# Fourteen Strassen groups instead of ten in each feed-forward part, and half of the ordinary low halves summed by DMAs

## The chip, the cores and the metric

The kernel runs on one core of a Trainium2 chip. It is written in Python against the engines: PE (TensorE) multiplies, PEld loads its stationary operand, DVE (VectorE) and ACT (ScalarE) do elementwise work, POOL (GpSimd) does a little of it and can begin DMAs, SP (SyncE) begins all other DMAs. Engines run their own instruction lists in order and wait for each other through semaphores. The metric is the device time of one execution in microseconds (us), lower is better.

## The reference

The reference is a two-layer block on 256 tokens of 2048 features in float32. Each layer has a mixer (the first a convolution and pooling mixer, the second a short-convolution mixer) and a feed-forward part:

```python
def swiglu(h, w_gate, w_up, w_down):
    return (jax.nn.silu(h @ w_gate) * (h @ w_up)) @ w_down

def reference(...):
    h = x
    for i in range(DEPTH):                       # DEPTH = 2
        ...                                      # mixer i
        h = h + swiglu(rms_norm(h, ffn_norm[i]), w_gate[i], w_up[i], w_down[i])
    return rms_norm(h, final_norm)
```

`w_gate` and `w_up` are 2048 x 5632, `w_down` is 5632 x 2048. The two feed-forward parts hold most of the arithmetic, and the change touches only them.

## The kernel before

**Three matmuls for one.** Weights are float32. PE multiplies a reduced format (`float32r`), so each operand is cut in two: a high half (the value rounded to that format) and a low half (the value less its high half). A product is three matmuls of 256 columns: high by high, high by the low of the other, low by high. ACT writes a weight's high half (`nc.scalar.copy`, line 200), and the low half is a subtraction (line 201), done by DVE, or by POOL for some pieces of the first mixer. The activations' halves are made once, in `split`.

**Units, pieces, tokens.** All weights lie in one array in the order in which they are used. A weight block is 128 x 128. SP loads units of 16 blocks, 1 MB, into four staging buffers `w` (pool `wst`, `fetch`, line 189). A unit of the ordinary kind ("P") is cut into pieces of 8 blocks, and `prepare` makes the two halves of a piece into the pool `whl`, which has five buffers named `hi` and five named `lo`. `advance` is called once for each token (one block's product, or one Strassen step): it prepares the pieces of the next three tokens that begin a piece (`LOOK`), and fetches one unit beyond.

**Strassen groups.** The 44 chunks (128 columns each) of gate and up are computed in two ways. An ordinary chunk takes 16 blocks of gate and 16 of up, three matmuls a block. A group takes two chunks, both of gate and up, by a seven-product scheme over 2 x 2 quarters: four units of weights, 14 steps each, three matmuls a step (lines 742 to 744, into the banks `s0` to `s3`). Of such a unit ("S") four parts are prepared (512, then three times 1024 columns), and DVE also makes three combinations of the quarters in place (lines 225 to 227). At the end of a product `combine` adds up the banks on DVE, and at the end of a group `turned` turns the result back with four transposes on PE (line 697) and writes it to `y`. The combinations of the activations are made at the start of a part by `s_forms`, from `h` through a tile `form` into `sf`.

**Sections and windows.** The 44 chunks are done in six sections, `SECTIONS`: pairs of (groups, ordinary chunks). In window w, section w of gate and up is computed, and the down projection of section w - 1 runs beside it; `merged` lays the steps of a window among its ordinary blocks in runs of 14. A seventh window holds the last section's down projection alone. With ten groups a part has 1472 ordinary blocks and 560 steps.

**What sets the order.** The program is written token by token, and a list scheduler then orders each engine's instructions; so an engine's order differs from the program's. A buffer of a pool is free when its last reader is done, and whoever fills it next waits for that: ACT waits for PE before it writes a `hi`, SP waits for DVE before it loads a `w`.

## Time and profile before

| | |
|---|---|
| median of 3 runs | 2032.01 us (2030.86 to 2033.54) |
| the profiled execution | 2031.89 us, its span 2030.0 us |
| PE, DVE, ACT, POOL busy | 98%, 82%, 56%, 10% of the span |
| mean granted clock of PE | 0.995 |
| bytes read from HBM | 391.39 MB, 194 GB/s over the span |
| feed-forward parts | about 250 to 941 us and 1306 to 1998 us |

In the rows of the trace, a line such as `L201 DVE ... x768 | 936.3, 1235 | 219.5 <-ACT hi L200` gives the line of the kernel, the engine, the operation, what is written from what, how many times, then the busy us and the mean ns of one, then the idle us of the engine just before them and who ended most of it. The rows of a stage give for each engine its busy us and the number of its instructions, then the granted clock, the mean busy share of the 16 DMA engines, and GB/s. Rows of DMA issues give the size of one and the median time from issue to landing. In the order of an engine's instructions a row has the line, the operation, what is written from what with buffer numbers, the size, and in brackets the semaphores it waits for (PE_49 is PE's, DMAHW those of DMAs begun by SP, DMASW those of DMAs begun by POOL).

### The profile page before, as it was taken

The page shows a single profiled execution, that of the slowest core. Times are in us where ns is not written, and L with a number is a line of the kernel's source. Part 1 is how long each engine was busy: PE and PEld are TensorE (multiplying, and loading weights), DVE is VectorE, ACT ScalarE, POOL GpSimd, SP SyncE. Part 2 cuts the span into 40 slices and gives each one's busy share as a digit, 9 for nine tenths or more (in the row PEclk, how much of TensorE's full clock was granted, in tenths as well). Part 3 has the DMA queues.
Part 4 walks back from the last instruction along what each step waited for, and adds up shares of the span by engine and source line. Part 5 has one row for each costly group of instructions (what it writes and reads, how often), then busy time and mean ns, then how long its engine had stood idle before and what let it go on. Part 6 is the DMA issues. An engine that isn't in the chain of part 4 may idle for free.

```text
span 2030.0 us, 41535 instructions
## 1 busy us (share of the span) xinstructions
PE 1996.3 (98%) x17410; PEld 1989.2 (98%) x17410; DVE 1664.1 (82%) x2326; ACT 1129.0 (56%) x1476; POOL 194.5 (10%) x180
## 2 busy tenths in 40 slices
PE   8999999999999999999999999999999999999997
PEld 8999899999999999999999999999999999999997
DVE  6998787888888888888766666788888888889875
ACT  7786675555555555556444445565555555555545
POOL 2996200000000000002000001100000000000002
PEclk9999999999999999999999999999999999999999
DMA  8555445454555545555555555545455454555552
GB/s 332 188 185 192 149 176 198 175 220 187 208 208 183 212 185 210 208 197 186 200 187 196 200 188 195 200 166 209 186 204 213 183 213 186 204 191 198 216 188 83
DMA packets 56922, 396.15 MB, mean 195 GB/s; under 512 B 6432, under 2 KB 7200, under 8 KB 9760
## 3 DMA queue, kind: packets, MB, share of 16 engines
q1 hardware_dynamic: 56736, 393.52, 52.5%
q8 instruction: 136, 2.23, 0.4%
q14 instruction: 50, 0.41, 0.1%
HBM read 391.39 MB, written 2.10 MB: 194 GB/s over the span
## 4 chain that ended last, share of the span: by engine, by line
PE 90%; DVE 7%; ACT 1%; DMA 1%; issue 1%; SPq 0%; POOL 0%; DVEq 0%; ACTq 0%; POOLq 0%
PE acc L289 24%; PE acc L290 23%; PE acc L291 23%; PE s L744 6%; PE s L742 6%; PE s L743 6%; DVE lo L201 2%; DVE side L513 1%; DVE side L515 1%; PE acc L697 0%; DMA rows<-in_xtok 0%; DMA h<-in_xT 0%; DVE h L782 0%; DVE xs L316 0%; ACT hi L200 0%
## 5 line engine op out<-in xcount | busy, mean ns | idle before, releaser
L200 ACT CAST hi<-w 128x1024 fp32r<-128x1024 f32 (+2 forms) x900 | 897.2, 1012 | 746.3 <-PE acc L290 431.9
L201 DVE TENSOR_TENSOR lo<-w,hi 128x1024 fp32r<-128x1024 f32 (+2 forms) x851 | 989.5, 1181 | 237.4 <-ACT hi L200 222.3
L289 PE MATMUL acc<-xs,hi 128*128 128x256 f32 x2816 | 777.2, 277 | 5.3 <-ACT hi L200 4.2
L290 PE MATMUL acc<-xs,hi 128*128 128x256 f32 x2816 | 775.7, 276 | 0.0
L291 PE MATMUL acc<-xs,lo 128*128 128x256 f32 x2816 | 772.7, 276 | 0.1
L289 PEld LDWEIGHTS acc<-xs,hi 128*128 128x128 f32 x2816 | 529.6, 188 | 6.2 <-ACT hi L200 4.8
L290 PEld LDWEIGHTS acc<-xs,hi 128*128 128x128 f32 x2816 | 529.8, 188 | 0.1
L291 PEld LDWEIGHTS acc<-xs,lo 128*128 128x128 f32 x2816 | 527.6, 188 | 0.6 <-DVE lo L201 0.5
L289 PE MATMUL acc<-y,hi 128*128 128x256 f32 x1408 | 389.0, 277 | 1.7 <-ACT y L699 1.3
L290 PE MATMUL acc<-y,hi 128*128 128x256 f32 x1408 | 388.2, 276 | 0.4 <-DVE y L700 0.4
L291 PE MATMUL acc<-y,lo 128*128 128x256 f32 x1408 | 386.7, 275 | 0.0
L289 PEld LDWEIGHTS acc<-y,hi 128*128 128x128 f32 x1408 | 264.2, 188 | 2.9 <-ACT y L699 1.8
L290 PEld LDWEIGHTS acc<-y,hi 128*128 128x128 f32 x1408 | 264.4, 188 | 0.9 <-DVE y L700 0.9
L291 PEld LDWEIGHTS acc<-y,lo 128*128 128x128 f32 x1408 | 263.9, 188 | 0.0
L422 POOL TENSOR_TENSOR sumsq<-sumsq,sq 128x256 f32<-128x256 f32 x56 | 52.6, 939 | 1553.1 <-ACT sq L420 1552.6
L743 PE MATMUL s<-hi,sf 128*128 128x256 f32 x640 | 175.7, 275 | 0.0
L742 PE MATMUL s<-hi,sf 128*128 128x256 f32 x640 | 175.7, 275 | 0.0
L744 PE MATMUL s<-lo,sf 128*128 128x256 f32 x640 | 171.8, 276 | 0.0
L744 PE MATMUL s<-lo,xs 128*128 128x256 f32 x480 | 132.5, 276 | 2.4 <-DVE lo L201 2.4
L742 PE MATMUL s<-hi,xs 128*128 128x256 f32 x480 | 132.6, 276 | 1.3 <-ACT hi L200 1.3
L743 PE MATMUL s<-hi,xs 128*128 128x256 f32 x480 | 132.2, 275 | 0.0
L201 POOL TENSOR_TENSOR lo<-w,hi 128x1024 fp32r<-128x1024 f32 x49 | 119.7, 2466 | 37.6 <-ACT hi L200 36.7
(163 smaller groups left out, 2310.4 us busy)
## 6 DMA issues: line engine op xcount, KB each, us to landing
w<-in_wall SPq DMA_DIRECT2D x365, 1024.0 KB, 4.9
w<-in_wall SPq DMA_DIRECT2D x7, 512.0 KB, 7.9
rows<-in_xtok SPq DMA_DIRECT2D x2, 1024.0 KB, 7.8
h<-in_xT SPq DMA_DIRECT2D x7, 256.0 KB, 7.2
out<-res SPq DMA_DIRECT2D x2, 512.0 KB, 2.8
out<-res SPq DMA_DIRECT2D x2, 384.0 KB, 2.7
v<-in_vec SPq DMA_DIRECT2D x1, 260.0 KB, 6.6
h<-in_xT SPq DMA_DIRECT2D x2, 128.0 KB, 2.3
```

Of the source, the lines that this page charges most:

```text
L200: nc.scalar.copy(hi, src)
L201: engine.tensor_tensor(out=lo, in0=src, in1=hi, op=ALU.subtract)
L289: nc.tensor.matmul(acc, hi, x[:, :T], start=first, stop=False)
L290: nc.tensor.matmul(acc, hi, x[:, T:], start=False, stop=False)
L291: nc.tensor.matmul(acc, lo, x[:, :T], start=False, stop=last)
L422: nc.gpsimd.tensor_tensor(out=self.sums[0], in0=self.sums[0], in1=sq, op=ALU.add)
L513: nc.vector.scalar_tensor_tensor(out=dst, in0=src, scalar=wt, in1=dst, op0=ALU.mult, op1=ALU.add)
L515: nc.vector.tensor_tensor(out=side, in0=side, in1=prods.pop((c, k)), op=ALU.add)
L742: nc.tensor.matmul(acc, xh, hi, start=first, stop=False, skip_group_check=True)
L743: nc.tensor.matmul(acc, xl, hi, start=False, stop=False, skip_group_check=True)
L744: nc.tensor.matmul(acc, xh, lo, start=False, stop=last, skip_group_check=True)
```

## The change

Four things change together, all in the feed-forward parts:

- `SECTIONS` holds 14 groups and 16 ordinary chunks in place of 10 and 24, in sections of 7, 5, 8, 8, 8 and 8 chunks. A part has 1216 ordinary blocks and 784 steps.
- Of each ordinary unit of 16 blocks that begins within a stated range of a part (`SUMMED`: from its 49th token to the end of its sixth window), the second piece gets its low half in another way. When the first piece is prepared, ACT writes minus the rounded weights into the `lo` buffer (`AF.Copy`, scale -1), and POOL begins a DMA that adds the weights to it (`accum_op=ALU.add`). The high half is cast when the piece itself is due. There are 65 such units in each part, 130 in all; the other low halves stay as they were.
- There are six `lo` buffers in place of five (also for the pieces of the first mixer that had a low buffer of their own).
- `s_forms` uses a quarter of one `w` staging buffer for each of its tiles, in place of the tile `form`.

```diff
-SECTIONS = ((1, 8), (2, 2), (2, 6), (2, 2), (2, 4), (1, 2))
+SECTIONS = ((1, 5), (2, 1), (2, 4), (3, 2), (3, 2), (3, 2))
...
+FFN_TOKENS = sum(len(w) for w in WINDOW_KINDS)
+SUMMED = sum(len(w) for w in WINDOW_KINDS[:-1])
+SUMMED = [range(at + 48, at + SUMMED) for at in (M0_BLOCKS, M0_BLOCKS + FFN_TOKENS + M1_BLOCKS)]
...
-    relief = []
+    relief, early = [], {}
...
         if spare:
-            hi, lo = (banks["spare"].tile([P, W_ROOM], F32R, name=x)[:, SPARE_AT : SPARE_AT + n] for x in ("hi", "lo"))
+            hi = banks["spare"].tile([P, W_ROOM], F32R, name="hi")[:, SPARE_AT : SPARE_AT + n]
         else:
-            hi, lo = (whl.tile([P, W_ROOM], F32R, name=x)[:, at : at + n] for x in ("hi", "lo"))
+            hi = whl.tile([P, W_ROOM], F32R, name="hi")[:, at : at + n]
+        lo = whl.tile([P, W_ROOM], F32R, name="lo", bufs=6)[:, at : at + n]
         nc.scalar.copy(hi, src)
         engine.tensor_tensor(out=lo, in0=src, in1=hi, op=ALU.subtract)
...
-            ready[key] = halves_of(w[:, o * P : (o + n) * P], 0, n * P, engine, key[1] in SPARE and i % 6 == 5)
+            src = w[:, o * P : (o + n) * P]
+            if u in early:
+                hi = whl.tile([P, W_ROOM], F32R, name="hi")[:, : n * P]
+                nc.scalar.copy(hi, src)
+                ready[key] = hi, early.pop(u)
+                return
+            if o == 0 and UNITS[u][3] == 2 * PIECE and any(UNITS[u][0] in x for x in SUMMED):
+                early[u] = lo = whl.tile([P, W_ROOM], F32R, name="lo", bufs=6)[:, : PIECE * P]
+                nc.scalar.activation(lo, w[:, PIECE * P :], AF.Copy, scale=-1.0)
+                nc.gpsimd.dma_start(lo, w[:, PIECE * P :], accum_op=ALU.add)
+            ready[key] = halves_of(src, 0, n * P, engine, key[1] in SPARE and i % 6 == 5)
             return
...
-    def s_forms(room, norm, fp, k):
-
-        f = fp.tile([P, 4, P], F32, name="form")
+    def s_forms(room, norm, scratch, k):
+
+        f = scratch[:, k % 4 * 4 * P : (k % 4 + 1) * 4 * P].rearrange("p (q t) -> p q t", q=4)
...
+            scratch = wst.tile([P, 16 * P], F32, name="w")
             for k in range(8):
-                later("wait", "form", partial(s_forms, sf, norm, fp, k))
+                later("wait", "form", partial(s_forms, sf, norm, scratch, k))
```

In the changed file the subtraction stands on line 205, the negation on 232, the DMA on 233, the three matmuls of a block on 303 to 305 and those of a Strassen step on 757 to 759.

## The prediction

> **What bounds the kernel now.** I read the head of the page first, then the chain that ended last, then the busy time by stage (the two feed-forward parts are 250 to 941 and 1306 to 1998 us, with the short-convolution mixer between them).

> ```profile
> span 2030.0 us, 41535 instructions
> PE 1996.3 (98%) x17410; PEld 1989.2 (98%) x17410; DVE 1664.1 (82%) x2326; ACT 1129.0 (56%) x1476; POOL 194.5 (10%) x180
> PE 90%; DVE 7%; ACT 1%; DMA 1%; issue 1%; SPq 0%; POOL 0%; DVEq 0%; ACTq 0%; POOLq 0%
> ```

> ```profile
> core 0: us, PE busy (x) PEld busy (x) DVE busy (x) ACT busy (x) POOL busy (x), PEclk, DMA share, GB/s
> 250.00:941.00 691.00, 687.12 (x6022) 685.27 (x6021) 591.27 (x793) 379.69 (x459) 1.99 (x2) 1.00 0.53 198
> 941.00:1306.00 365.00, 364.68 (x3206) 363.86 (x3206) 256.80 (x346) 170.17 (x213) 28.01 (x43) 1.00 0.54 191
> 1306.00:1998.00 692.00, 688.41 (x6036) 686.81 (x6036) 592.22 (x792) 378.86 (x461) 1.53 (x2) 1.00 0.53 195
> 430.00:600.00 170.00, 170.00 (x1498) 170.00 (x1497) 145.11 (x183) 92.79 (x109) 0.00 (x0) 1.00 0.54 200
> ```

> PE is the bound: 90% of the last chain, and idle for 4 us of each feed-forward part. In the undisturbed stretch of the last row a matmul takes a turn every 170/1498 = 0.1135 us. So the number of matmuls sets these parts, as long as nothing that a matmul reads comes late. DVE has about 14% to spare there (591 of 691), ACT 45%, POOL is empty, and the 16 DMA engines are half busy. The profiled execution took 2031.89 us; its span is 2030.0, and 1.9 us lie around it. It is within 0.2 us of the median of the runs, so the sum is made on 2031.9.

> **The change, part by part.**

> (1) Matmuls. A group does two chunks of gate and up in 56 steps x 3 = 168 matmuls, where the ordinary way takes 2 x 2 x 16 x 3 = 192. Four more groups in each part, eight in all, remove 8 x 24 = 192 matmuls: 192 x 0.1135 = **-21.8 us**. Each group adds four transposes, in two pairs:

> ```profile
> 622.93 0.28 PE L744 MATMUL s<-lo,sf 128*128 128x256 f32 x1
> 623.05 0.38 PE L697 MATMUL acc<-v 128*128 128x128 f32 x2
> 623.19 0.36 PE L289 MATMUL acc<-xs,hi 128*128 128x256 f32 x1
> 623.39 0.28 PE L290 MATMUL acc<-xs,hi 128*128 128x256 f32 x1
> ```

> From 623.05 to 623.39 a pair and one matmul take 0.34; less the matmul's 0.11 a pair costs 0.23. 16 pairs are **+3.7 us**. PE alone would thus gain 18.1 us.

> (2) DVE. The rows that price it (and ACT):

> ```profile
> L201 DVE TENSOR_TENSOR lo<-w,hi 128x1024 fp32r<-128x1024 f32 x768 | 936.3, 1235 | 219.5 <-ACT hi L200 205.2
> L200 ACT CAST hi<-w 128x1024 fp32r<-128x1024 f32 x817 | 846.6, 1052 | 681.2 <-PE acc L290 399.5 <-DVE w L227 190.1 <-PE s L743 64.9
> L225 DVE TENSOR_TENSOR w<-w 128x1024 f32<-128x1024 f32 x80 | 97.5, 1219 | 1.1
> L201 DVE TENSOR_TENSOR lo<-w,hi 128x512 fp32r<-128x512 f32 x81 | 55.6, 687 | 17.2 <-ACT hi L200 16.3
> L226 DVE TENSOR_TENSOR w<-w 128x512 f32<-128x512 f32 x80 | 54.8, 685 | 0.9
> L200 ACT CAST hi<-w 128x512 fp32r<-128x512 f32 x81 | 50.4, 622 | 64.4 <-PE acc L290 32.3 <-DMA w<-in_wall 21.8 <-issue 5.5
> L443 DVE TENSOR_TENSOR gate<-acc,rstd 128x256 f32<-128x256 f32 x72 | 30.3, 421 | 17.5 <-PE acc L291 17.3
> L700 DVE TENSOR_TENSOR y<-acc,y 128x512 fp32r<-128x512 f32 x20 | 13.7, 684 | 2.3 <-ACT y L699 2.3
> L724 DVE SCALAR_TENSOR_TENSOR v<-v,rtok,c 128x256 f32<-128x256 f32 x20 | 9.5, 476 | 0.0
> L708 DVE TENSOR_TENSOR c<-s,a 128x256 f32<-128x256 f32 x20 | 8.3, 417 | 0.0
> ```

> A Strassen unit costs DVE 3 x 1.235 + 0.687 + 1.219 + 2 x 0.685 = 6.98 us; 32 more units are +223. Eight more groups add seven sums of 0.42, two products of 0.48 and a 0.68 each, +36. Removed are 64 low halves of ordinary pieces that no longer exist and the 130 that DMAs now sum, 194 x 1.235 = -240, and four operations of 0.42 for each of 16 ordinary chunks, -27. The sum is -8 us: DVE is as full as before. Without the DMAs it would be 161 us fuller, of some 200 that it is idle in both parts, and in the last three sections 137 us of its rows would stand against 122.6 us of matmuls; the DMAs are the cover under which the matmuls may be dropped. With them, DVE has 122 us of rows there for the 1080 matmuls of a section; rows of DVE overlap by about 0.08, and the same sum for a middle section of before gives 110 of 114 where the stages show 86% busy, so I expect 90%. ACT gains 130 negations (as a cast, 1.05) and the units' casts, about 195 us on 1129: not a bound. Of DVE's bursts at the turn of a group I expect what is there now, under 1 us at some turns; I leave it at nothing in the sum and 4 us in the range.

> (3) The new chain: ACT negates half a unit, POOL begins a DMA, the DMA reads the half and the negation and writes the sum, PE waits. POOL's order in the change, at the start of the second part (L436 is the running sum of squares, L233 the DMA):

> ```order
> L436 TENSOR_TENSOR sumsq_15454<-sumsq_15454,sq_16363 128x256 [waits Activation_49,Pool_49]
> L233 DMA lo_16575<-w_16479 128x1024 [waits DMASW2_49,DMAHW3_49,DVE_49,Activation_49]
> L233 DMA lo_16656<-w_16582 128x1024 [waits DMASW3_49,DMAHW4_49,DVE_49,Activation_49]
> L233 DMA lo_16743<-w_16663 128x1024 [waits DMASW7_49,DMAHW5_49,DVE_49,Activation_49]
> L233 DMA lo_16906<-w_16812 128x1024 [waits DMASW4_49,DMASW0_49,DMAHW7_49,DVE_49,Activation_49]
> ```

> Where POOL stood empty there are now 65 DMAs in each part and nothing else among them, so a DMA waits on POOL for nobody; the issue also has no queue of SP to pass. What matters is how long the chain may take. ACT in the fifth section of the second part, change:

> ```order
> L204 CAST hi_21901<-w_21811 128x1024 [waits DMAHW2_49,PE_49,Activation_49]
> L227 CAST hi_21919<-w_21811 128x1024 [waits PE_49,Activation_49]
> L204 CAST hi_21933<-w_21905 128x512 [waits DMAHW3_49,PE_49]
> L232 ACTIVATE lo_21898<-w_21811 128x1024 [waits DMASW1_49]
> L783 ACTIVATE gate_21884<-gate_21884 128x256 [waits DVE_49]
> ```

> and before, at a like place (an ordinary unit's two casts between the casts of Strassen units):

> ```order
> L200 CAST hi_21258<-w_21155 128x1024 [waits DMAHW5_49,PE_49,Activation_49]
> L200 CAST hi_21276<-w_21155 128x1024 [waits DVE_49,PE_49]
> L200 CAST hi_21304<-w_21262 128x512 [waits DMAHW6_49,DVE_49,PE_49]
> L200 CAST hi_21336<-w_21262 128x1024 [waits PE_49]
> L200 CAST hi_21369<-w_21262 128x1024 [waits DVE_49,PE_49,Activation_49]
> ```

> The negation stands behind three casts, the first of which waits for a buffer. There are five buffers of high halves, and the one it gets is that of `hi_21793`. PE in the change frees it in the third row here:

> ```order
> L305 MATMUL acc_21761<-xs_75,lo_21772 128x256
> L303 MATMUL acc_21761<-xs_75,hi_21793 128x256
> L304 MATMUL acc_21761<-xs_75,hi_21793 128x256
> L305 MATMUL acc_21761<-xs_75,lo_21772 128x256
> L757 MATMUL s1_21635<-hi_21856,sf_16435 128x256 [waits Activation_49]
> ```

> and needs the sum 70 matmuls later, in the fourth row here:

> ```order
> L757 MATMUL s1_21635<-hi_21951,sf_16435 128x256
> L758 MATMUL s1_21635<-hi_21951,sf_16435 128x256
> L759 MATMUL s1_21635<-lo_21952,sf_16435 128x256
> L305 MATMUL acc_21887<-xs_75,lo_21898 128x256 [waits DMASW5_49]
> L303 MATMUL acc_21887<-xs_75,hi_21919 128x256
> ```

> PE works in order, so everything behind that row stands while it waits. That ACT is tied to freed buffers, and how soon it starts, the trace shows (the wait's total, and one instance):

> ```profile
> ACT hi L200 <- PE acc L290: 431.9, 324, 4.0
> 505.16 0.28 PE L290 MATMUL acc<-xs,hi 128*128 128x256 f32 x1
> 505.53 1.05 ACT L200 CAST hi<-w 128x1024 fp32r<-128x1024 f32 x1 [0.56 <-PE acc L290]
> ```

> It starts 0.37 after the freeing matmul starts. So 70 x 0.1135 = 7.94 us, less 0.37 and 3 x 1.05 + 0.62 on ACT, leaves 3.8 us from the end of the negation to PE's need. I counted this at all 130 sums, with PE never standing (DVE's waits on ACT left out, so it is generous): the median is 4.4 us, 24 sums have less than 3.3, 62 less than 4, and 52 over 5 (nearly all of these before or after the Strassen-heavy sections). If the chain from negation to PE takes L, PE stands for the sum of what is missing: 9 us in all for L = 3.2, 17 for 3.5, 34 for 3.9, 83 for 4.64, 149 for 5.5, 366 for 8. The waits do not melt into each other, since the next casts are tied to matmuls that the wait has pushed back too.

> No DMA that adds is in the trace. The nearest rows:

> ```profile
> q1 hardware_dynamic: 56736, 393.52, 52.5%
> w<-in_wall SPq DMA_DIRECT2D x365, 1024.0 KB, 4.9
> w<-in_wall SPq DMA_DIRECT2D x7, 512.0 KB, 7.9
> out<-res SPq DMA_DIRECT2D x2, 512.0 KB, 2.8
> v<-in_vec SPq DMA_DIRECT2D x1, 8.0 KB, 1.7
> ```

> Lower end: a plain 512 KB store, 2.8. Upper end: 512 KB behind other loads, 7.9. In between: the fixed part is that of the 8 KB load, 1.7; 393.52 MB took 52.5% of 2030 us, 2.71 us a MB. A sum reads 2 x 512 KB, 1.05 MB, so 2.84. 1.7 + 2.84 = 4.54, near the row that moves as many bytes (4.9). With 0.1 for the two hand-overs I take **L = 4.64: +83 us**.

> [...]

> (4) The rest: forms that are made in a weight buffer take one of four at the start of a part, and SP's loads of ordinary units now wait for a DMA in place of DVE. Loads stand ready long before:

> ```profile
> SPq L193 <- DVE lo L201: 1314.8, 273, 16.0
> ```

> SP waits 1315 us for free buffers, so a buffer freed 4 us later costs nothing. If it did, ACT's casts would show waits for `w`. Bytes from the DMAs: 130 x 2.84/2030 puts the share at about 0.7, not a bound.

> Sum: 2031.9 - 21.8 + 3.7 + 83 = 2096.8, **2097 us**.

> **Rivals.** First, *the sums are in time*: read and added as fast as a plain copy, 1.7 + 1.42 + 0.1 = 3.2, so PE stands 9 us: 2031.9 - 18.1 + 9 = 2023, down to 2016 if bursts help. For it: the 2.8 us store. Against: 32 sums have under 3.5 us even so. It decides below L = 3.4 (13.8 us of waits). [...] Second, *a draw*: L from 3.4 to 3.7 gives waits of 14 to 24 us against 18 gained, 2028 to 2036. Third, *transfers in each other's way*: an ordinary unit's sum begins while a 1 MB load is running, as with the 7.9 us row; at L = 6 PE stands 190 us, 2204. Against: loads fill only half of the time. That the matmuls are not saved is no rival: 160 fewer rows stand on PE.

> **How the numbers follow.** Late sums as forecast 0.53, in each other's way 0.07, in time 0.29, a draw 0.11. Slower 0.60, faster 0.29, same 0.11 (a measurement of this kernel can tell about 0.2%, 4 us, from no change). The forecast's own range is L = 3.9 to 5.5, 2048 to 2163. The whole range reaches down to the sums in time, 2016, and stops at 2165, leaving out most of the third rival and the best of the first.

> **What would show it.** Right: matmuls of L305 as waiters with an idle time before them put down to the DMA of `lo`, some 1 us each in 70 or more places of the last three sections, PE's busy share in the parts down to about 95%, landing of the 512 KB sums at 4.5 us or more. Wrong: landing of 3.3 us or less and 5900 matmuls in some 680 us of a part; or DVE's idle time gone in the last three sections while sums land early, which would make the bound DVE, and not the sums. The PE term is wrong if matmuls fall by other than 160.

## The result, and the profile after

The changed kernel takes 2261.7 us (median; 2253.3 to 2271.8) against 2032.2 for the kernel before: a ratio of 1.113, 95% interval 1.110 to 1.117. It is slower, as forecast, but by 229 us where 65 were forecast, outside the range of 2016 to 2165.

The head of the page after, its chain that ended last (by engine, then by line), its DMA queues and its DMA issues (the last number is the median us from issue to landing):

```profile
span 2251.4 us, 41942 instructions
PE 2062.1 (92%) x17250; PEld 2036.6 (90%) x17250; DVE 1661.9 (74%) x2372; ACT 1275.0 (57%) x1670; POOL 311.4 (14%) x310
...
q0 software_dynamic: 18720, 68.17, 15.4%
...
PE 55%; DMA 26%; issue 10%; DVE 7%; ACT 2%; SPq 0%; DVEq 0%; POOLq 0%; ACTq 0%; POOL 0%
DMA lo<-w 24%; PE acc L305 16%; PE acc L303 15%; PE acc L304 15%; DVE lo L205 3%; PE s L757 3%; PE s L759 3%; PE s L758 3%; DVE side L527 1%; DVE side L529 1%; ACT hi L204 1%; DMA w<-in_wall 1%; DMA rows<-in_xtok 0%; DMA h<-in_xT 0%; PE acc L712 0%
...
lo<-w POOLq DMA_DIRECT2D x130, 512.0 KB, 8.7
```

There are 160 matmuls less, DVE's work is what it was (1664.1 before), and a quarter of the chain is now the sums: 8.7 us each in the median. Three groups of instructions and the waits of PE show where they are felt. L305 is the low-half matmul, L233 POOL's issue of a sum:

```profile
L305 PE MATMUL acc<-y,lo 128*128 128x256 f32 x1408 | 407.4, 292 | 93.7 <-DMA lo<-w 93.6
L305 PE MATMUL acc<-xs,lo 128*128 128x256 f32 x2304 | 643.0, 281 | 52.1 <-DMA lo<-w 51.8
L233 POOL DMA_DIRECT2D lo<-w x130 | 112.0, 862 | 1417.6 <-ACT lo L232 855.4
```

```profile
PEld acc L305 <- DMA lo<-w: 162.1, 82, 4.3
PE acc L305 <- DMA lo<-w: 145.5, 78, 4.1
```

By stage (first part, mixer, second part):

```profile
250.00:1050.00 800.00, 719.48 (x5950) 708.05 (x5950) 597.19 (x820) 457.17 (x567) 65.56 (x75) 0.97 0.73 215
1050.00:1420.00 370.00, 370.00 (x3265) 369.95 (x3264) 259.16 (x352) 170.97 (x211) 22.36 (x37) 1.00 0.52 189
1420.00:2220.00 800.00, 717.12 (x5889) 706.05 (x5889) 583.56 (x800) 450.25 (x557) 65.63 (x72) 0.96 0.72 211
```

The mixer runs as before; all is lost in the two parts. There PE stands for some 80 us each, and its granted clock, 1.00 before, is 0.97 and 0.96.

To count what was lost I took, for every matmul of a trace, the time from its start to the next start, less 0.114 us, where that is positive. The sum grows from 50.4 us to 289.5. That is 239 us; less 18 for the 160 matmuls that are gone, it is the 221 us by which the span grew. Split into gaps of over 0.3 us, by the matmul that ends them, and everything smaller:

| trace | us (median) | sums, landing | gaps at low halves | gaps at S pieces and turns | gaps elsewhere | smaller | at half clock |
|---|---|---|---|---|---|---|---|
| before | 2032 | - | 0.2 | 7.0 | 24.0 | 19.2 | 9.3 |
| the change | 2262 | 130, 8.7 | 159.5 | 18.9 | 26.2 | 84.9 | 122.2 |
| no sums | 2104 | - | 0.4 | 55.0 | 28.7 | 59.8 | 45.2 |
| ten groups, sums | 2125 | 170, 9.5 | 72.6 | 0.0 | 27.5 | 42.9 | 43.8 |
| loads held | 2148 | 130, 5.5 | 82.3 | 20.6 | 21.8 | 55.7 | 44.8 |
| copies | 2114 | 130, 6.3 | 55.2 | 19.0 | 23.2 | 47.6 | 38.2 |
| sums begun early | 2073 | 130, 9.5 | 26.2 | 18.7 | 25.2 | 38.4 | 23.0 |
| ten groups, early | 2062 | 170, 9.5 | 19.6 | 1.0 | 25.6 | 26.9 | 9.7 |

"Low halves" are those of ordinary pieces after 250 us, "turns" the transposes at a group's turn. The last column is the time in which the granted clock was 0.5, from 250 us to the last instruction (all 9.3 us of the kernel before lie after 2017 us, of the change 6.1 us after 2245); much of "smaller" is matmuls that took 0.21 us there instead of 0.11 (median from start to start in the change's trace). The change's 239 us are 159 of waiting for sums, 12 at S pieces and turns, 66 of slower matmuls, and 2 elsewhere.

**Why 8.7 us.** An instance, in order of time on ACT, SP and POOL (start, length):

```profile
969.42 1.06 ACT L232 ACTIVATE lo<-w 128x1024 fp32r<-128x1024 f32 x1
969.88 0.80 SPq L196 DMA_DIRECT2D w<-in_wall  x2
970.78 0.87 POOL L233 DMA_DIRECT2D lo<-w  x1 [9.97 <-ACT lo L232]
```

SP begins two 1 MB loads within the microsecond before the sum. In the transfers' records the first packet starts a median of 4.4 us after the issue (1.4 at the earliest), taken over the 113 sums that were issued after the one before had landed. In all 130 cases a load was in flight when 1.3 us had passed since the issue; a load was begun within the 2 us before 90 of the 130 issues, and two within the 3 us before 41. It is no chance that the loads come just then, as the waits of SP's queue show:

```profile
SPq L196 <- DMA lo<-w: 1069.4, 130, 11.5
SPq L196 <- DVE lo L205: 730.6, 169, 17.5
```

An ordinary unit's staging buffer is now freed by the sum that reads it. SP stands before that load until the sum has landed, and the Strassen unit's load is queued behind it. Then both go out together, and by then the next sum is due. The chain of waits has the sum before this one in the same state, followed at once by its matmul:

```profile
959.93 9.82 DMA lo<-w
969.79 0.38 PE acc L305
```

### The profile page after: what moved, and what is told of

Same layout as the page of the kernel before. It is cut to its first block, busy times and chain, and to the rows that moved or that the text cites. A ratio compares the mean times of both kernels' runs of the same rounds, so it can differ in the third digit from the quotient of the medians.

```text
span 2251.4 us, 41942 instructions
## 1 busy us (share of the span) xinstructions
PE 2062.1 (92%) x17250; PEld 2036.6 (90%) x17250; DVE 1661.9 (74%) x2372; ACT 1275.0 (57%) x1670; POOL 311.4 (14%) x310
## 3 DMA queue, kind: packets, MB, share of 16 engines
q1 hardware_dynamic: 56736, 393.52, 50.6%
q0 software_dynamic: 18720, 68.17, 15.4%
## 4 chain that ended last, share of the span: by engine, by line
PE 55%; DMA 26%; issue 10%; DVE 7%; ACT 2%; SPq 0%; DVEq 0%; POOLq 0%; ACTq 0%; POOL 0%
DMA lo<-w 24%; PE acc L305 16%; PE acc L303 15%; PE acc L304 15%; DVE lo L205 3%; PE s L757 3%; PE s L759 3%; PE s L758 3%; DVE side L527 1%; DVE side L529 1%; ACT hi L204 1%; DMA w<-in_wall 1%; DMA rows<-in_xtok 0%; DMA h<-in_xT 0%; PE acc L712 0%
## 5 line engine op out<-in xcount | busy, mean ns | idle before, releaser
L204 ACT CAST hi<-w 128x1024 fp32r<-128x1024 f32 (+2 forms) x834 | 801.8, 988 | 721.3 <-PE acc L304 342.9
L205 DVE TENSOR_TENSOR lo<-w,hi 128x1024 fp32r<-128x1024 f32 (+2 forms) x785 | 889.0, 1153 | 225.9 <-ACT hi L204 219.3
L305 PE MATMUL acc<-xs,lo 128*128 128x256 f32 x2304 | 643.0, 281 | 52.1 <-DMA lo<-w 51.8
L303 PE MATMUL acc<-xs,hi 128*128 128x256 f32 x2304 | 642.7, 280 | 8.3 <-ACT hi L204 4.6
L304 PE MATMUL acc<-xs,hi 128*128 128x256 f32 x2304 | 641.4, 279 | 0.0
L305 PE MATMUL acc<-y,lo 128*128 128x256 f32 x1408 | 407.4, 292 | 93.7 <-DMA lo<-w 93.6
L305 PEld LDWEIGHTS acc<-xs,lo 128*128 128x128 f32 x2304 | 438.3, 191 | 58.9 <-DMA lo<-w 58.4
L303 PEld LDWEIGHTS acc<-xs,hi 128*128 128x128 f32 x2304 | 439.9, 191 | 9.5 <-ACT hi L204 5.2
L304 PEld LDWEIGHTS acc<-xs,hi 128*128 128x128 f32 x2304 | 440.0, 191 | 0.1
L303 PE MATMUL acc<-y,hi 128*128 128x256 f32 x1408 | 404.6, 288 | 0.0
L304 PE MATMUL acc<-y,hi 128*128 128x256 f32 x1408 | 403.9, 287 | 0.0
L305 PEld LDWEIGHTS acc<-y,lo 128*128 128x128 f32 x1408 | 278.9, 199 | 103.8 <-DMA lo<-w 103.7
L233 POOL DMA_DIRECT2D lo<-w x130 | 112.0, 862 | 1417.6 <-ACT lo L232 855.4
L304 PEld LDWEIGHTS acc<-y,hi 128*128 128x128 f32 x1408 | 279.4, 198 | 0.0
L303 PEld LDWEIGHTS acc<-y,hi 128*128 128x128 f32 x1408 | 279.0, 198 | 0.0
L757 PE MATMUL s<-hi,sf 128*128 128x256 f32 x896 | 252.2, 282 | 6.7 <-ACT hi L204 6.7
L758 PE MATMUL s<-hi,sf 128*128 128x256 f32 x896 | 248.7, 278 | 0.0
L759 PE MATMUL s<-lo,sf 128*128 128x256 f32 x896 | 231.3, 278 | 1.8 <-DVE lo L205 1.8
L797 DVE TENSOR_TENSOR h<-acc,h 128x256 f32<-128x256 f32 x192 | 80.9, 422 | 173.7 <-PE acc L305 172.4
L759 PE MATMUL s<-lo,xs 128*128 128x256 f32 x672 | 186.4, 277 | 1.0
L757 PE MATMUL s<-hi,xs 128*128 128x256 f32 x672 | 186.7, 278 | 0.0
L758 PE MATMUL s<-hi,xs 128*128 128x256 f32 x672 | 186.5, 277 | 0.0
## 6 DMA issues: line engine op xcount, KB each, us to landing
w<-in_wall SPq DMA_DIRECT2D x365, 1024.0 KB, 5.1
lo<-w POOLq DMA_DIRECT2D x130, 512.0 KB, 8.7
w<-in_wall SPq DMA_DIRECT2D x7, 512.0 KB, 8.9
rows<-in_xtok SPq DMA_DIRECT2D x2, 1024.0 KB, 8.0
out<-res SPq DMA_DIRECT2D x2, 512.0 KB, 2.7
```

What stands on the lines that cost most here:

```text
L204: nc.scalar.copy(hi, src)
L205: engine.tensor_tensor(out=lo, in0=src, in1=hi, op=ALU.subtract)
L233: nc.gpsimd.dma_start(lo, w[:, PIECE * P :], accum_op=ALU.add)
L303: nc.tensor.matmul(acc, hi, x[:, :T], start=first, stop=False)
L304: nc.tensor.matmul(acc, hi, x[:, T:], start=False, stop=False)
L305: nc.tensor.matmul(acc, lo, x[:, :T], start=False, stop=last)
```

## The experiments

**Parts of the change alone.** First, 14 groups without sums (all low halves by DVE):

```diff
-            if o == 0 and UNITS[u][3] == 2 * PIECE and any(UNITS[u][0] in x for x in SUMMED):
+            if False:
```

> The changed kernel with its 14 groups, but every low half made by DVE as before (no negation, no DMA by GpSimd). If the DMAs carry the whole loss: 2031.9 - 18.1 = 2014 plus what DVE now lacks. By the prediction's rows DVE has 137 us of rows, about 123 once their overlap is taken off, for 122.6 us of matmuls in each of the last three sections, so 2014 to 2045. If the groups and sections themselves cost (rival): over 2100, with PE waiting for low halves of DVE.

Measured: 2103.8 us, ratio 1.034 (1.032 to 1.037). Page and waits of that run:

```profile
PE 2029.8 (96%) x17250; PEld 2005.5 (95%) x17250; DVE 1790.8 (85%) x2502; ACT 1151.0 (55%) x1540; POOL 199.6 (9%) x180
PE 75%; DVE 17%; ACT 3%; issue 3%; DMA 1%; SPq 0%; ACTq 0%; DVEq 0%
```

```profile
ACT hi L204 <- DVE w L241: 360.8, 95, 6.8
PEld acc L712 <- DVE v L739: 34.9, 23, 2.7
PEld s L757 <- ACT hi L204: 22.5, 53, 1.6
```

DVE is late at the S pieces and at the turns (55 us of gaps where the change has 19). So the sums do relieve DVE, and the 14 groups without relief are already 72 us slower than the kernel before. The rival's time is met (over 2100), but not its place: the gaps at ordinary low halves are 0.4 us.

Second, the sums on the old ten groups:

```diff
-SECTIONS = ((1, 5), (2, 1), (2, 4), (3, 2), (3, 2), (3, 2))
+SECTIONS = ((1, 8), (2, 2), (2, 6), (2, 2), (2, 4), (1, 2))
```

> The ten groups and sections of before, with the sums (170 of them, since there are more ordinary units). If the DMAs carry the loss as in the changed kernel, where PE lost 239 us with 130 sums, 1.8 us each: about 2032 + 313 = 2345; if the lead is longer where ordinary blocks stand closer, less, 2130 at the least. If the groups carry it: within 10 us of 2032. Landing of the sums near 8.7 us again.

Measured: 2125.0 us, ratio 1.046 (1.044 to 1.048). 170 sums land in 9.5 us and cost 73 us of gaps; the time lies a little under the 2130 that was expected as the least. No gap is left at the S pieces and turns, so the change's 19 us there belong to its sections. The two parts alone cost 72 and 93 us, together 229. They make each other dearer. Call a sum's budget the work that PE has left between the end of the negation and the matmul that needs the sum: the matmuls between them in the trace, at 0.1135 us each. On ten groups the median budget is 10.3 us (none of 170 under 6), in the change 7.9 (12 of 130 under 5).

**Loads out of the way.** The load of a Strassen unit is made to wait for the landing of the sum three units earlier:

```diff
+            if UNITS[u][1] == "S" and u - 3 in sums:
+                tc.add_manual_dep(load, sums[u - 3].name, ...)
```

> The changed kernel, with each load of a Strassen unit made to wait for the landing of the sum of the ordinary unit three units earlier, so that no 1 MB load is begun just ahead of a sum. Theory Q (a sum's first packet waits behind the packets of a load begun just before): landing falls from 8.7 us to 4.6 to 6, PE's waits for sums fall by more than half, time 2080 to 2150. Theory R (adding is slow in itself) and theory G (GpSimd is slow to write the descriptors): landing stays over 8 us, time 2230 or more (more still if loads come late: waits of ACT for w).

Measured: 2148.2 us, ratio 1.057 (1.055 to 1.060).

```profile
lo<-w POOLq DMA_DIRECT2D x130, 512.0 KB, 5.5
```

```profile
PEld acc L307 <- DMA lo<-w: 84.5, 68, 4.8
```

The landing falls from 8.7 to 5.5 us and 114 us come back. 34 sums now find no load in flight; their first packet starts 1.43 us after issue and they land after 4.55. This shows the queueing: the sums' bytes and number are the same. The writing of descriptors that theory G supposes stands in no row of these traces.

**Adding against copying.** The same DMAs copy instead of adding; the low half of these pieces is then the weights themselves.

```diff
-                nc.gpsimd.dma_start(lo, w[:, PIECE * P :], accum_op=ALU.add)
+                nc.gpsimd.dma_start(lo, w[:, PIECE * P :])
```

> The changed kernel with DMAs that copy instead of add; the low half is then the weights themselves, so this part of the computation is changed. One source is read, not two. Theory R: data time of a DMA falls from 2.67 us to about 1.4, landing to under 7 us, time under 2190. Theory Q: landing falls by no more than the data time, 1.3 us, to 7.4 or more, since the first packet still comes some 4 us after the issue; time 2200 to 2260.

Measured: 2113.8 us, ratio 1.040 (1.037 to 1.044).

```profile
q0 software_dynamic: 18720, 68.17, 8.8%
...
L233 POOL DMA_DIRECT2D lo<-w x130 | 68.9, 530 | 1320.0 <-ACT lo L232 760.2
...
lo<-w POOLq DMA_DIRECT2D x130, 512.0 KB, 6.3
```

A copy takes 8.8% of 2106.8 us over 130, 1.43 us of all 16 engines; the adding DMA takes 15.4% of 2251.4, 2.67. Its issue on POOL takes 530 ns instead of 862. Theory R's figures hold (1.43 us of data, landing under 7 us, time under 2190), theory Q's do not. But the longer data time is not alone: a copy still lands only after 6.3 us, though the fastest landed in 2.96, and its first packet comes 3.25 us after issue, where the change has 4.4. So much of its time is standing behind loads, and shorter sums shorten that too.

**Smaller loads.** Each load is begun as up to eight DMAs of 256 columns:

```diff
+            for c in range(0, n * P, 256):
+                c1 = min(c + 256, n * P)
+                nc.sync.dma_start(w[:, c:c1], whole[:, c:c1])
```

> As the change, with each load of weights on SP begun as DMAs of 256 columns, up to eight (128 KB each) in place of one of 1 MB. Theory that a sum waits until the whole DMA ahead of it is through, since turns go from DMA to DMA: its first packet comes after one of the eight, landing under 7.5 us, time under 2210. Rival (the sum waits behind all that stands queued, or shares the engines packet by packet): landing 8 to 9.5 us and time within 1.5% of the change's 2262; worse if SP's own issuing becomes late.

Measured: 2230.7 us, ratio 1.097 (1.095 to 1.100).

```profile
PE 46%; DMA 27%; SPq 9%; issue 9%; DVE 6%; ACT 3%; POOL 0%; DVEq 0%; ACTq 0%; POOLq 0%
...
w<-in_wall SPq DMA_DIRECT2D x2951, 128.0 KB, 3.6
lo<-w POOLq DMA_DIRECT2D x130, 512.0 KB, 6.6
```

The landing falls to 6.6 us as the first theory said, the first packet to 2.0 us after issue (median, taken as above). The time does not follow, and lies in the rival's range: the gaps at low halves fall only from 159 to 111 us, and SP itself (9% of the chain, by 2951 issues) and late loads (15%, against 1% in the change) take the place of part of the wait. The edit changes the packets too (each row of a load is 1 KB, not 8 KB), so whether a sum stands behind a whole DMA or behind its long rows isn't told apart.

**Beginning earlier.** The sum of a unit is begun one piece sooner, at the second piece of the unit before:

```diff
+            if o == PIECE and u in early:
...
+                begin(next(v for v in range(u + 1, len(UNITS)) if UNITS[v][1] != "S"))
```

> As the change, but the sum of an ordinary unit is begun one piece earlier, with the piece before its unit's first one, so that in the order of instructions it has a median of 11.0 us (least 5.2) between the end of the negation and its first matmul, where the change has 4.4. Lateness theory (the 179 us that TensorE lost at the low halves that DMAs make are landing less budget, so 8.7 - 4.4 in the median, and the half clock follows these waits): the waits at these halves fall under 25 us, the landing may stay at 8 to 9 us, the windows at half clock fall under 15, and the time is 2030 to 2075 us (2014 that the matmuls leave, 20 to 60 for VectorE in the sections of three groups). Rival (the sums' traffic or the six lo buffers, each held some 8 us longer, limit the stages): the wait moves to ScalarE and VectorE for buffers, and the time stays above 2110.

Measured: 2073.2 us, ratio 1.020 (1.018 to 1.022).

```profile
PE 2006.3 (97%) x17250; PEld 1987.2 (96%) x17250; DVE 1659.8 (80%) x2372; ACT 1270.0 (61%) x1670; POOL 311.3 (15%) x310
...
lo<-w POOLq DMA_DIRECT2D x130, 512.0 KB, 9.5
```

```profile
PEld acc L312 <- DMA lo<-w: 26.9, 25, 2.4
```

The decisive run. The sums are slower than in the change (9.5), and 188 of the 229 us come back, because their budget is now 11.2 us in the median by the trace, where the change has 7.9. What set the time was lateness against PE's need, not the load on the DMA engines, whose mean share in the parts rose from 0.73 to 0.81. Left over against 2014 are 26 us of gaps at sums (a little more than expected), 12 us more at S pieces and turns than before, and 19 us of slower matmuls; the time at half clock is 14 us longer than before.

**GpSimd subtracts.** The 130 low halves are made by POOL instead of a DMA:

```diff
+            if o == PIECE and UNITS[u][3] == 2 * PIECE and any(UNITS[u][0] in x for x in SUMMED):
+                engine = nc.gpsimd
```

> As the change, but the second piece's low half of the same 130 units is subtracted by GpSimd itself (the row of the kernel before: 2466 ns for one of 128x1024) instead of by a DMA; VectorE's and ScalarE's work stays near the change's (no negation). Theory that the loss is all in the DMA's 8.7 us: 2.5 us behind the high half is less than the DMA, no queue behind loads, 2030 to 2075 us and no granted clock below 0.98. Rival (the sections of three groups are too full for any second summer; GpSimd slows VectorE, or stands in line for the high half): above 2090.

Measured: 2205.3 us, ratio 1.085 (1.083 to 1.086); the rival. Groups of DVE and POOL with shapes kept apart, first the change, then this run:

```profile
L205 DVE TENSOR_TENSOR lo<-w,hi 128x1024 fp32r<-128x1024 f32 x670 | 816.1, 1234 | 213.0 <-ACT hi L204 206.6
L205 DVE TENSOR_TENSOR lo<-w,hi 128x512 fp32r<-128x512 f32 x113 | 77.4, 685 | 12.2 <-ACT hi L204 12.0
```

```profile
L205 DVE TENSOR_TENSOR lo<-w,hi 128x1024 fp32r<-128x1024 f32 x670 | 892.2, 1349 | 197.2 <-ACT hi L204 190.7
L205 DVE TENSOR_TENSOR lo<-w,hi 128x512 fp32r<-128x512 f32 x113 | 200.6, 1775 | 2.6 <-ACT hi L204 2.6
L205 POOL TENSOR_TENSOR lo<-w,hi 128x1024 fp32r<-128x1024 f32 x179 | 498.2, 2792 | 1141.4 <-ACT hi L204 965.3
```

The same DVE instructions take longer: the subtractions of 128x512 go from 685 to 1775 ns, DVE from 1662 to 1886 us for 2372 instructions, and PE waits 99 us at S pieces and turns. All 111 of DVE's low-half subtractions that took over 1.4 us here overlap one of POOL's. Those of 128x512 take 679 ns in the mean where none of POOL's runs (53 of them) and 2743 where one does (60), and these 60 end 0.55 us after POOL's does, so they seem to stand until it is done.

**The clock.** Ten idle matmuls stand before each wait for a sum:

```diff
+        if fill.get("now"):
+            idle = ps_st.tile([P, P], F32, name="idle", tag="st")
+            with tc.issue_after(mm.ins):
+                for _ in range(10):
+                    mm = nc.tensor.matmul(idle, fill["ones"], fill["ones"], start=True, stop=True)
```

> As the change, with ten idle matmuls of 128x128 (about 0.125 us each at full clock, 1.25 us together) on TensorE before the first matmul of each low half that a DMA sums. They take up waiting that is there anyway; worked out from the 82 gaps over 0.25 us of the change's trace, they add 74 us where the gap is shorter than 1.25 us and leave 70 us of gap. Clock theory (the half clock, about 59 us of slow matmuls, comes from TensorE standing idle): the 32 windows at half clock fall to under 12 and the time is 2270 to 2300 us. Rival (the half clock has another cause, the transfers for one, or hangs on waiting shorter than what is left): the windows stay above 22, and the time is 2320 to 2345.

Measured: 2302.5 us, ratio 1.132 (1.131 to 1.134).

```profile
PE 2271.2 (99%) x19850; PEld 2266.9 (99%) x19850; DVE 1683.5 (73%) x2372; ACT 1295.0 (56%) x1670; POOL 311.1 (14%) x310
...
PE acc L305 19%; PE acc L306 19%; PE acc L315 18%; PE idle L311 12%; PE s L768 7%; PE s L769 7%; PE s L767 7%; DMA lo<-w 1%; DVE side L537 1%; DVE side L539 1%; DVE lo L205 1%; PE acc L313 1%; PE acc L722 1%; DMA rows<-in_xtok 0%; ACT hi L204 0%
```

```profile
250.00:1050.00 800.00, 797.97 (x6998) 797.56 (x6998) 585.72 (x791) 450.32 (x540) 59.34 (x68) 1.00 0.73 206
```

An idle matmul turned out to be two records long, so ten take 12% of 2299.7 us over 130, 2.1 us; 1.25 was the author's estimate, and the expected times are off by that. The question is answered by the clock: with PE hardly standing (1 us of gaps at low halves), and the transfers as dense as in the change (0.73), the clock is 1.00 in the parts, and of the change's 32 stretches at half clock 2 are left. So the half clock came from PE's waiting, and not from the transfers. The kernel with all waits filled is nearly the one expected of a PE without waits: 2014 plus 276 for the idle matmuls is 2290.

**Combinations.** Early sums on the old ten groups; early sums for every second unit; early sums with loads held; and twelve groups with every second unit.

```diff
-SECTIONS = ((1, 5), (2, 1), (2, 4), (3, 2), (3, 2), (3, 2))
+SECTIONS = ((1, 8), (2, 2), (2, 6), (2, 2), (2, 4), (1, 2))    # ten groups
+SECTIONS = ((1, 8), (2, 2), (2, 4), (2, 2), (3, 2), (2, 2))    # twelve groups
-                if v in early or UNITS[v][3] != 2 * PIECE or ...
+                if v in early or UNITS[v][2] // 16 % 2 or UNITS[v][3] != 2 * PIECE or ...    # every second unit
```

> The ten groups and sections of the kernel before, with the change's sums by DMAs, each begun one piece earlier as in the run with early sums (170 of them; median budget 9.8 us, least 4.1, 24 under 5). With late sums this layout took 2125 us. Layout theory (what the run with early sums and 14 groups still lost, 2073 against 2014, comes from the fuller sections of three groups): 2030 to 2052 us here, waits of TensorE for the sums under 20 us. Traffic theory (it comes from the sums themselves, their traffic and the lo buffers they hold): 2060 to 2090 us.

Measured: 2061.8 us, ratio 1.014 (1.012 to 1.016), at the edge of the traffic theory. 20 us of gaps at the sums remain, and 1 us at S pieces and turns. By the trace no budget is under 8.6 us (the median is 12.5), but some sums land up to 12.7 us after their negation.

> 14 groups, early sums for every second ordinary unit only (66 in place of 130; VectorE sums the other half). None took 2104 us with VectorE late at the S pieces and the turns of groups, all 130 took 2073 with 27 us of waiting for sums. If both losses shrink with their share, the time lies under both, 2045 to 2070; if VectorE's lateness sets in with the first units given back to it (VectorE over 83% of the span), 2075 to 2100.

Measured: 2062.7 us, ratio 1.015 (1.013 to 1.017), as if both losses shrank with their share; DVE is over the 83% of the other expectation, without its time.

```profile
PE 2000.2 (97%) x17250; PEld 1982.2 (97%) x17250; DVE 1720.6 (84%) x2436; ACT 1209.6 (59%) x1606; POOL 257.8 (13%) x246
```

66 sums leave 9 us of gaps at low halves and, with DVE at 84%, 24 at S pieces and turns.

> 14 groups, all 130 sums early, and the load of a Strassen unit held until the sum three units earlier has landed, as in the run with loads held. Queue theory: the landing falls from 9.5 to under 7 us, the waits for sums from 27 to under 10 us, 2050 to 2068 us. Rival: budgets of 11 us leave nothing for it to gain and the held loads come late for ScalarE and VectorE, 2072 to 2110.

Measured: 2106.7 us, ratio 1.037 (1.034 to 1.041). The landing stayed at 9.5 us: with the sums moved, the rule holds the loads at a time that puts 127 of 130 sums beside one again. It tells only that held loads come late (36 us of gaps at S pieces and turns); the queue theory isn't tested by it.

> 12 groups (sections of 10, 6, 8, 6, 8, 6 chunks, one of them of three groups) and early sums for every second ordinary unit (76). TensorE has 80 matmuls less than the kernel before, 9 us. If what is lost goes with the sections of three groups and with VectorE's share, 2025 to 2045 us, and a version near or under the kernel before; if the sums cost wherever they stand, 2045 to 2070.

Measured: 2066.6 us, ratio 1.017 (1.016 to 1.019): 19 us of gaps at 76 sums, 19 at S pieces and turns, as the second expectation had it. No version with sums reached the kernel before.

## Why the prediction was right and wrong

(1) **Matmuls: right.** 160 fewer records; at 0.114 us they are the 18 us of the sum.

(2) **DVE: the amount right, the turns mis-sized.** DVE's busy time went from 1664.1 to 1661.9 us, forecast -8. The turns of groups and S pieces were put at nothing in the sum and 4 us in the range; gaps there rose by 12 us (7.0 to 18.9), and they are 19 to 21 us with copies, with loads held and with sums begun early too, and 0 or 1 where sums run on ten groups. Without the sums, the cover named in the prediction, they are 55 us, and DVE is busy for 129 us more than in the change, where the prediction had 161 by its rows.

(3) **The chain of the sum: the step that failed, by its term L.** The mechanism was right: PE stands at L305 for sums that land after its need, 82 times. The price of the DMA by itself was right as well: 1.7 + 2.84 = 4.54 us, and the sums without a load in flight (with loads held) landed in 4.55; the change's have 2.67 us of data by the queue's share. But no sum of the change was by itself. From the end of the negation to the landing took 9.0 us in the median (8.7 of it after the issue) in place of L = 4.64; its cause is the third rival, transfers in each other's way, which had a chance of 0.07 because "loads fill only half of the time". That share is a mean. The loads are not spread over it: the change itself ties them to the sums.

(3b) **The time that the chain may take: counted too short.** The table gives, by its own steps, 149 us at L = 5.5 and 366 at 8. The change lost 159 us with L = 9.0, and the run with loads held 82 with 5.9. The median of 4.4 us, on which the table rests, is not what PE had: by the change's trace it is 7.9 us, with 12 sums under 5 us, not 78. The prediction's own instance shows why:

```profile
1911.88 2.00 ACT L204 CAST hi<-w 128x1024 fp32r<-128x1024 f32 x2
1913.79 1.04 ACT L227 CAST hi<-w 128x1024 fp32r<-128x1024 f32 x1
1914.29 0.28 PE L304 MATMUL acc<-xs,hi 128*128 128x256 f32 x1
1914.74 0.62 ACT L204 CAST hi<-w 128x512 fp32r<-128x512 f32 x1
1915.26 1.05 ACT L232 ACTIVATE lo<-w 128x1024 fp32r<-128x1024 f32 x1
1922.16 0.28 PE L759 MATMUL s<-lo,sf 128*128 128x256 f32 x1
1925.42 0.58 PE L305 MATMUL acc<-xs,lo 128*128 128x256 f32 x1 [2.98 <-DMA lo<-w]
```

The matmul at 1914.29 is the one that frees `hi_21793`, 70 before the one that waits for the sum. The two casts of 1024 columns that the prediction puts behind it (the second of the first row, and that of L227) had begun by then, so they cannot have been waiting for that buffer; only the cast of 512 columns and the negation come after it. The negation ended at 1916.31, and PE was ready for the sum at 1922.3: 6.0 us, not 3.8. "The waits do not melt into each other" is neither borne out nor refuted by this: the trace's 7.9 us have in them what PE's own waits gave the negations, and how much that is was not measured.

So two errors worked against each other, and that the wait term stayed near the 190 us that the third rival had for L = 6 is luck. So is, in part, the direction. With the change's budgets, L = 4.64 would cost some 7 us (an estimate from the trace, and a low one, since PE's waits lengthen its budgets); 2031.9 - 21.8 + 3.7 + 7 is 2021, near the first rival. The forecast of "slower" came from a budget that was too short; the change was slower because of L.

(3c) **A term was missing.** The slow matmuls, 66 us of which most is the half clock, are in none of the cases. Without them the change would lie near 2200.

(4) **"A buffer freed 4 us later costs nothing": wrong.** SP had 1315 us of waiting to spare, so its loads themselves were not late. But the sums free the buffers now (1069 us of SP's waiting), and this puts the next two loads where the next sum starts. What the edit moved past the queue was not the load's landing but its timing.

A sum took 2.67 us of data and a copy 1.43, with 18720 packets and 68.17 MB in the queue's row of either run. The 2 x 512 KB behind the prediction's 2.84 us stand in no row: that reading two sources is what makes a sum longer was the author's estimate, and the runs show the times alone. The first rival had the copy's rate; even the copy, at 2114 us, would not have brought it.

The signs named as proof held (waits at L305, landing over 4.5 us, 160 matmuls), though the 82 waits are of 2 us each and not of 1. The sign "95% busy in the parts" did not: it is 90%.

## What to carry to other kernels

Price a new transfer by who else is on the engines at the moment when it starts, not by the mean share (a sum landed in 4.55 us with no load in flight, in 8.7 in the change); and ask what its own completion sets free, since that is what will run beside the next one. A transfer that is slow but begun early enough costs little: one piece of head start was worth 188 us, more than making it faster in any way that was tried. When you count a chain in the order of instructions, find for each of them which buffer it really waits for. And count waits on PE twice: once as waiting (159 us at the sums here) and once as the clock that follows (113 us more than before at 0.50).

## What was not expected of the hardware

```profile
627.32:630.73 3.41, 1.50 (x12) 1.50 (x13) 1.22 (x1) 3.41 (x4) 0.00 (x0) 1.00 0.39 74
630.73:634.14 3.41, 3.41 (x19) 3.41 (x18) 1.05 (x2) 1.34 (x3) 0.00 (x0) 0.50 0.73 279
845.78:849.19 3.41, 1.57 (x14) 1.38 (x13) 2.19 (x4) 1.75 (x2) 0.00 (x0) 1.00 0.92 195
849.19:852.60 3.41, 2.25 (x19) 2.25 (x20) 1.68 (x2) 3.10 (x4) 0.02 (x1) 1.00 0.37 89
```

In the first window no matmul ran for 2.04 us in all (a matmul counted as 0.114 us from its start; the busy times in the rows go by modelled ends), and the whole next window is at 0.50, busy throughout with 19 matmuls. In the third it was 2.00 us, and the clock stays. I divided the change's trace, from 250 us to the final norm, into such windows, on the grid on which its clock changes: after all 31 full-clock windows with 2.04 us or more without a matmul came one at half clock, after none of some 515 with 2.01 or less. In seven other traces with waits (no sums, ten groups, loads held, copies, early, subtracting on GpSimd, small loads) the border lies between 1.99 and 2.07 us as well, with 78 halved windows; the kernel before has one of 2.03 and none halved. In the change most of these windows held one wait of about 2 us. That it is the sum that counts is shown by the run without sums: two of its windows had 1.99 and 2.02 us in all with no wait over 1.2 us, and the next was halved, while the change's window with a single wait of 2.01 us was not followed by one.

**A sum's packets came behind those of a load that started first.** The first packet came 1.4 us after issue with no load in flight (the run with loads held), 4.4 in the change, 2.0 with loads in eight parts (medians). In the change's instance at 970.78 the engines moved only the loads' packets until 975.57, when the first of the sum's began. Why wasn't settled.

**An adding DMA costs POOL more to issue** than a copy of the same shape: 862 ns (the change) against 530 (the copies).
